# Output product of the first block: the first attention's part in all four blocks ahead of the second's

## The chip, the core and the metric

The kernel runs on one core of a Trainium2 chip. The metric is the device time of one execution in microseconds (us). The core has five engines that run side by side, each through its own list of instructions in order: TensorE (PE, matrix products), VectorE (DVE), ScalarE (ACT), GpSimd (POOL) and SyncE (SP, which issues the transfers). They wait for each other by semaphores.

## The reference

The reference is two transformer blocks in float32 over 256 positions of width 1024. The change lies in the first block:

```python
h = rmsnorm(x, g_mix_pre[l])
proj = h @ w_in[l]
...
y_fox = forgetting_attention(...)            # first attention, 512 columns
y_chk = chunked_relpos_attention(...)        # second attention, 512 columns
y = jnp.concatenate([rmsnorm(y_fox.reshape(B, S, D_FOX), g_fox_out[l]),
                     rmsnorm(y_chk.reshape(B, S, D_CHK), g_chk_out[l])], axis=-1)
x = x + rmsnorm(y @ w_out[l], g_mix_post[l])
h = rmsnorm(x, g_mem_pre[l])
mem_n = rmsnorm(mem, g_mem_kv[l])
y = memory_cross_attention(h, mem_n, w_mq, w_mk, w_mv, w_mo)   # four heads of width 256
x = x + rmsnorm(y, g_mem_post[l])
```

A feed-forward part (1024 to 4096 to 1024) follows, and then the second block (a gated delta rule, a sparse attention, a feed-forward part).

## The kernel before

The 256 positions are two halves of 128, since an engine works on 128 partitions. Every float32 product is made of three products in a faster format: both operands are split into a high and a low part (`whi`, `wlo` for weights, `xhi`, `xlo` for activations), and `mm3` adds high x high, high x low and low x high in one bank of TensorE's accumulator. Weights come in units of 512 KB (class `Part`): SyncE loads a unit into `raw`, ScalarE casts it to `whi`, VectorE subtracts to `wlo`. A unit of w_out is 256 rows by 512 columns, so w_out has eight units; the first four give columns 0 to 511 of the output, the others columns 512 to 1023. In each four, the first two hold the rows of the first attention and the last two those of the second.

The order on each engine is that in which the Python code writes the instructions. The main line writes products; after each `mm3` or so it calls `tick`, which lets side chains (generators, class `Side`) write their next piece. When a chain may go on is decided by the planner's own clock (`k.clock`, `k.at`, `k.done`: estimated costs). A chain that the planner thinks is ready is written; `k.finish(...)` writes what is left of the named chains at once, whatever the clock says. `part` and `drop` take the next unit or let one go, and write casts and splits of later units up to a limit (`pump`); `k.held` counts the units kept for the other half.

Around the change the main line writes, in this order: `gemm_t` for the memory keys; the first half of the memory values (`gn`, columns 0 to 511); the output product (`gs`, the loop that the change rewrites); the second half of the memory values (`gn` again, four units, 48 matmuls); `k.finish(*st.values())` (line 1024); the query product `gemm_t(k, ht, D, mq_evac)` (`gt`, 192 matmuls); `k.finish(*[st[i] for i in range(3)])` (line 1071); the memory output product (`mo`).

In the output product the two attentions are not yet normalized: their parts of a block go to two banks, and `out_sum` (line 988) scales and adds them: `y` = bank of the first attention x its factor (ScalarE), then + bank of the second x its factor (VectorE). When a half has both column blocks, `out_post` (line 996) starts `chain_post` (line 467): sums of squares of y on ScalarE (`junk`), `yg` = y x gain, the factor `rs` on GpSimd, `x` = yg x rs + old x, sums of squares of x (`junk`), `xg` = x x gain, `rs`, `xg` x rs, and then eight transposes on TensorE in two banks (`tb`), each cast to `xhi` by ScalarE and split to `xlo` by VectorE. This is the query product's moving operand, and that needs both halves.

The loop before goes half by half and block by block: first attention, second attention, first attention, second attention. The second attention's chain is finished (`k.finish(s_chk)`) after the first two units of the first block. In the query product each of the four heads starts a chain `mem_head` (line 1030) when its columns are there: for each half the scores (`ms`), maximum, exponential, sum, scaling (`mp`), two transposes (`tb`), a copy (`mpt`); then the head's output (`ops`), cast and split.

Of the kernel before, what the change touches and what calls it, by code (L numbers as in the profile page):

```python
# [16 lines left out]
P = 128  # L17
S = 256
D = 1024
# [343 lines left out]
    return [Part(w, r, 2, c0 + c, wd) for c in range(0, ncols, wd) for r in range(0, D, S)]  # L363


def gemm_t(k, xt, ncols, evac):

    for i in range(ncols // 256):
        ps = k.bank((P, 2, S), "gt")
        for m in range(2):  # L370
            p = k.part()
            for kt in range(KT):
                k.mm3(ps[:, m, :], p.at(kt, 0, P), xt.x(kt), kt == 0, kt == KT - 1)
                k.tick()
            if m == 1 and not evac(i, ps):
                k.put()
            k.tick()
# [11 lines left out]
def gemm_n_inter(k, xt, evac, width=512, nb=1):  # L389

    ps = [[k.bank(name="gn") for _ in range(nb)] for _ in range(2)]
    for i in range(4):
        p = k.part()
        for half in range(2):
            mm_n(k, ps[half], xt, half, p, 2 * i, width)
            if i == 3 and not evac(half, ps[half]):
                k.put(nb)
    k.tick()
# [134 lines left out]
def ffn(k, xt, before_b, evac, last=None):  # L533
# [24 lines left out]
    def up(c):  # L558
        u_tiles(c)
        uh, ul = us[c]  # L560

        def ev(i, ps):
            r = k.t2([P, 2, S], name="r")
            sl = slice(2 * i, 2 * i + 2)
            nc.scalar.activation(r, ps, AF.Relu)
            nc.vector.tensor_tensor(r, r, r, op=OP.mult)
            split(k, uh[:, sl], ul[:, sl], r)
        gemm_t(k, xt, 512, ev)
# [98 lines left out]
def join(sides):  # L667

    if sides:
        yield list(sides)  # L670
# [20 lines left out]
def block1(k, x, mem, w_in, b_fgt, rel, g_fox_out, g_chk_out, w_out, g_mix_pre, g_mix_post,  # L691
           g_mem_kv, w_mq, w_mk, w_mv, w_mo, g_mem_pre, g_mem_post, w_ff1, w_ff2, g_ff_pre,
           g_ff_post, next_gain, xt_next, before_ffn=None):
    nc = k.nc

    x0 = [k.t4([P, D], name="x0") for _ in range(2)]
    grow = k.t4([1, D], name="grow")
# [12 lines left out]
    for half in range(2):  # L710
        xg.append(k.t4([P, D], name="xg"))
        ss, r = k.small(1, "ss"), k.small(1, "rs")
# [4 lines left out]
    u = k.units  # L717
# [91 lines left out]

    fq, ev = qk_evac(0.125)  # L810
    gemm_t(k, ht, 512, ev)
    mt = XT(k)
    s_m = [k.add(chain_norm(k, mt, half, m0[half], gkv)) for half in range(2)]
    fk, ev = qk_evac(1.0)
    gemm_t(k, ht, 512, ev)


    yt = XT(k)
# [143 lines left out]
    s_chk = k.add(chk())  # L962
# [23 lines left out]
    st = {}  # L986

    def out_sum(half, j, banks, y):

        yield banks + [rso]  # L990
        yy = y[:, j * 512:j * 512 + 512]
        nc.scalar.activation(yy, banks[0], AF.Copy, scale=rso[:, 0, half:half + 1])
        nc.vector.scalar_tensor_tensor(yy, banks[1], rso[:, 1, half:half + 1], yy, op0=OP.mult, op1=OP.add)
        k.put(2)

    def out_post(half, sums, y):
        yield from join(sums)
        yield from chain_post(k, half, [y[:, :512], y[:, 512:]], gpo, x0[half], x1[half], gmp, ht, nbanks=0)

    parts = []  # L1000
    for half in range(2):
        y, sums = k.t4([P, D], name="y"), []
        for j in range(2):
            banks = []
            for i in range(4):
                if half == 0:
                    parts.append(k.part())
                    k.held += 1
                else:
                    k.drop()  # L1010
                if i % 2 == 0:
                    banks.append(k.bank(name="gs"))
                if (half, j, i) == (0, 0, 2):
                    k.finish(s_chk)
                p = parts[4 * j + i]
                for r in range(2):
                    k.mm3(banks[i // 2], yt.x(2 * i + r, half), p.at(r, 0, 512), i % 2 == 0 and r == 0,
                          i % 2 == 1 and r == 1)
                    k.tick()
            sums.append(k.add(out_sum(half, j, banks, y), rank=-1))  # L1020
        st[half] = k.add(out_post(half, sums, y), rank=-1)
        k.tick()
    gemm_n_inter(k, mt, lambda half, ps: nc.scalar.copy(mv[half][:, 1], ps[0]))
    k.finish(*st.values())

# [36 lines left out]
    st = {}  # L1062
# [12 lines left out]
    parts = {}  # L1075
# [863 lines left out]
```

## Time and profile before

| | us |
|---|---|
| median of 3 runs | 886.81 (886.73 to 886.85) |
| the profiled execution | 886.64 |
| its span, first to last instruction | 884.9 |
| TensorE busy | 871.4 (98%) |
| VectorE busy | 597.7 (68%) |
| ScalarE busy | 456.5 (52%) |
| GpSimd busy | 88.9 (10%) |

TensorE has 89% of the chain of waits that ended last, VectorE 5%, ScalarE 4%. The output product takes 144 to 167 us of the span, the second half of the memory values 167 to 178, the query product with most of the heads 180 to 216. A matmul's end in the profile is modelled and its successor starts before it, so the pace of a series is read from the starts. In a timeline row stand the start, the time busy, the engine, the line of the code, the operation, the result and the operands, the sizes, the count, and in brackets the idle time before it with what ended it. Most vector instructions are written through one helper, so their line is 96; matmuls are written in line 212, transposes in line 225.

### The profile page before, as it was taken

What the parts mean: (1) busy time and instruction counts of PE and PEld (TensorE: products, weight loads), DVE (VectorE), ACT (ScalarE), POOL (GpSimd) and SP (SyncE); (2) the same over time, 40 slices, a digit from 0 to 9 for tenths busy, and PEclk for the clock granted to TensorE, in tenths of its full rate; (3) what the DMA queues carried; (4) which work ended last, traced back from release to release, by engine and by line L of the source; (5) the groups of instructions that cost most, each with busy time, mean ns of one, the idle gap of its engine ahead of it and who ended that gap; (6) DMA issues with size and microseconds to landing.
All of it is one profiled execution on the core that took longest, in us unless ns stands there. A gap on an engine that the chain in (4) does not pass through costs nothing.

```text
span 884.9 us, 14527 instructions
## 1 busy us (share of the span) xinstructions
PE 871.4 (98%) x5664; PEld 766.8 (87%) x5664; DVE 597.7 (68%) x1074; ACT 456.5 (52%) x775; POOL 88.9 (10%) x144
## 2 busy tenths in 40 slices
PE   8999999999999999999999999999999999999998
PEld 7978987888789999998798899988987889999987
DVE  5686674865687556554769999878579785555541
ACT  6665644653476444442656665554564654444440
POOL 3100000200020000000100038800010000000000
PEclk9999999999999999999999999999999999999999
DMA  8982455472387666654651677385126587666621
GB/s 265 303 220 78 138 180 176 144 259 80 94 240 221 207 196 191 189 191 145 170 161 49 191 172 198 89 245 168 49 72 197 169 248 217 178 194 187 196 82 47
DMA packets 163381, 150.32 MB, mean 170 GB/s; under 512 B 21105, under 2 KB 128241, under 8 KB 163314
## 3 DMA queue, kind: packets, MB, share of 16 engines
q1 hardware_dynamic: 162738, 148.36, 56.7%
q10 hardware_dynamic: 576, 1.05, 0.4%
q8 instruction: 44, 0.72, 0.3%
q14 instruction: 23, 0.19, 0.1%
HBM read 147.56 MB, written 1.84 MB: 169 GB/s over the span
## 4 chain that ended last, share of the span: by engine, by line
PE 89%; DVE 5%; ACT 4%; issue 1%; DMA 0%; POOL 0%; DVEq 0%; ACTq 0%; POOLq 0%
PE gt L212 33%; PE acc L212 20%; PE gs L212 13%; PE gn L212 9%; PE tb L225 3%; PE mo L212 3%; DVE wlo L96 2%; ACT whi L96 1%; PE s L212 1%; ACT junk L96 1%; PE ops L212 1%; ACT p L96 1%; PE ms L212 1%; PE o L212 1%; DVE Z L96 1%
## 5 line engine op out<-in xcount | busy, mean ns | idle before, releaser
L96 DVE TENSOR_TENSOR wlo<-raw,whi 128x1024 fp32r<-128x1024 f32 (+1 forms) x263 | 315.2, 1224 | 107.2 <-ACT whi L96 106.6
L96 ACT CAST whi<-raw 128x1024 fp32r<-128x1024 f32 (+1 forms) x264 | 268.2, 1047 | 81.6 <-DMA raw<-in_w_in_dram 29.3
L212 PE MATMUL gt<-xhi,whi 128*128 128x256 f32 x832 | 238.5, 287 | 0.2 <-ACT xhi L96 0.2
L212 PE MATMUL gt<-xlo,whi 128*128 128x256 f32 x832 | 233.6, 281 | 0.3 <-DVE xlo L96 0.3
L212 PE MATMUL gt<-xhi,wlo 128*128 128x256 f32 x832 | 233.2, 280 | 0.0
L212 PEld LDWEIGHTS gt<-xhi,whi 128*128 128x128 f32 x832 | 156.7, 188 | 4.1 <-issue 3.2
L212 PEld LDWEIGHTS gt<-xlo,whi 128*128 128x128 f32 x832 | 156.8, 188 | 1.0 <-DVE xlo L96 0.5
L212 PEld LDWEIGHTS gt<-xhi,wlo 128*128 128x128 f32 x832 | 156.7, 188 | 0.0
L212 PE MATMUL acc<-whi,ul 128*128 128x512 f32 (+1 forms) x288 | 106.2, 369 | 0.0
L212 PE MATMUL acc<-wlo,uh 128*128 128x512 f32 (+1 forms) x288 | 106.2, 369 | 0.0
L212 PE MATMUL acc<-whi,uh 128*128 128x512 f32 (+1 forms) x288 | 106.1, 368 | 0.0
L212 PE MATMUL gs<-whi,xhi 128*128 128x512 f32 (+1 forms) x208 | 80.4, 387 | 0.5 <-ACT xhi L96 0.5
L212 PE MATMUL gs<-whi,xlo 128*128 128x512 f32 (+1 forms) x208 | 79.0, 380 | 0.4 <-DVE xlo L96 0.4
L212 PE MATMUL gs<-wlo,xhi 128*128 128x512 f32 (+1 forms) x208 | 78.7, 379 | 0.1
L212 PE MATMUL gn<-whi,xhi 128*128 128x512 f32 x160 | 67.3, 420 | 0.0
L212 PE MATMUL gn<-whi,xlo 128*128 128x512 f32 x160 | 63.0, 394 | 0.0
L212 PE MATMUL gn<-wlo,xhi 128*128 128x512 f32 x160 | 63.0, 394 | 0.0
L212 PEld LDWEIGHTS acc<-whi,ul 128*128 128x128 f32 x288 | 54.1, 188 | 9.8
L212 PEld LDWEIGHTS acc<-whi,uh 128*128 128x128 f32 x288 | 54.2, 188 | 9.6
L212 PEld LDWEIGHTS acc<-wlo,uh 128*128 128x128 f32 x288 | 54.1, 188 | 9.6
L96 DVE TENSOR_TENSOR r<-r 128x512 f32<-128x512 f32 x32 | 22.1, 690 | 58.4 <-ACT r L96 58.4
L96 ACT ACTIVATE r<-gt 128x512 f32<-128x512 f32 x24 | 14.4, 598 | 74.7 <-PE gt L212 74.7
(367 smaller groups left out, 1123.4 us busy)
## 6 DMA issues: line engine op xcount, KB each, us to landing
raw<-in_w_in_dram SPq DMA_DIRECT2D x84, 512.0 KB, 4.8
raw<-in_w_ff_dram SPq DMA_DIRECT2D x64, 512.0 KB, 5.0
raw<-in_w_mlp_up_dram SPq DMA_DIRECT2D x32, 512.0 KB, 5.7
raw<-in_w_mlp_down_dram SPq DMA_DIRECT2D x32, 512.0 KB, 4.3
raw<-in_w_out_dram SPq DMA_DIRECT2D x16, 512.0 KB, 3.8
raw<-in_w_mk_dram SPq DMA_DIRECT2D x8, 512.0 KB, 4.7
raw<-in_w_mv_dram SPq DMA_DIRECT2D x8, 512.0 KB, 3.6
raw<-in_w_mq_dram SPq DMA_DIRECT2D x8, 512.0 KB, 4.9
```

The lines of the kernel that those rows point to most:

```text
L96: f(*args, **kw)
L212: self.nc.tensor.matmul(out, lhsT, rhs, start=start, stop=stop)
L225: self.nc.tensor.transpose(out, in_, self.ident[:n, :n])
```

## The change

The loop over halves and blocks is now inside a loop over the two attentions: for the first attention (t = 0) all four pairs of half and column block, 48 matmuls, then `k.finish(s_chk)`, then for the second (t = 1) the same four. The banks of the first pass stay occupied until their sums. The eight units of w_out are loaded in the order of their new use (0, 1, 4, 5, 2, 3, 6, 7). A unit is held from its first half to its second, so four at a time instead of eight.

```diff
+def first_rows_first(units, w):
+
+    at = [i for i, u in enumerate(units) if u.src.tensor is w.tensor]
+    part = [units[i] for i in at]
+    for i, j in zip(at, (0, 1, 4, 5, 2, 3, 6, 7)):
+        units[i] = part[j]
...
     nc = k.nc
+    first_rows_first(k.units, w_out)
...
-    parts = []
-    for half in range(2):
-        y, sums = k.t4([P, D], name="y"), []
-        for j in range(2):
-            banks = []
-            for i in range(4):
-                if half == 0:
-                    parts.append(k.part())
-                    k.held += 1
-                else:
-                    k.drop()
-                if i % 2 == 0:
-                    banks.append(k.bank(name="gs"))
-                if (half, j, i) == (0, 0, 2):
-                    k.finish(s_chk)
-                p = parts[4 * j + i]
-                for r in range(2):
-                    k.mm3(banks[i // 2], yt.x(2 * i + r, half), p.at(r, 0, 512), i % 2 == 0 and r == 0,
-                          i % 2 == 1 and r == 1)
-                    k.tick()
-            sums.append(k.add(out_sum(half, j, banks, y), rank=-1))
-        st[half] = k.add(out_post(half, sums, y), rank=-1)
-        k.tick()
+
+    parts, banks, ys, sums = {}, {}, {}, {}
+    for t in range(2):
+        if t == 1:
+            k.finish(s_chk)
+        for half in range(2):
+            if t == 1:
+                ys[half], sums[half] = k.t4([P, D], name="y"), []
+            for j in range(2):
+                banks[t, half, j] = k.bank(name="gs")
+                for i in range(2):
+                    if half == 0:
+                        parts[t, j, i] = k.part()
+                        k.held += 1
+                    else:
+                        k.drop()
+                    for r in range(2):
+                        k.mm3(banks[t, half, j], yt.x(4 * t + 2 * i + r, half), parts[t, j, i].at(r, 0, 512),
+                              i == 0 and r == 0, i == 1 and r == 1)
+                        k.tick()
+                if t == 1:
+                    sums[half].append(k.add(out_sum(half, j, [banks[0, half, j], banks[1, half, j]], ys[half]),
+                                            rank=-1))
+            if t == 1:
+                st[half] = k.add(out_post(half, sums[half], ys[half]), rank=-1)
+            k.tick()
```

The change moves the instructions of the chains behind it as well, since the planner writes them when its clock says so. On VectorE, from the second sum of half 1 to the scaling before its transposes, stood this before (`x0_75`, `y_1865` and `xg_2033` are half 1's; `tb_1971` holds half 0's second four transposes):

```order
L96 TENSOR_TENSOR xlo_1791<-tb_1971,xhi_1789 128x4x128
L96 SCALAR_TENSOR_TENSOR y_1865<-gs_1951,rso_639,y_1865 128x512
L96 TENSOR_TENSOR wlo_2001<-raw_1910,whi_2000 128x1024
L96 TENSOR_TENSOR yg_2012<-y_1865,gain_1684 128x512 x2
L96 SCALAR_TENSOR_TENSOR x0_75<-yg_2012,rs_2020,x0_75 128x512 x2
L96 TENSOR_TENSOR xg_2033<-x0_75,gain_1686 128x512 x2
L96 TENSOR_TENSOR wlo_2037<-raw_1926,whi_2036 128x1024
L96 TENSOR_TENSOR wlo_2059<-raw_1943,whi_2058 128x1024
L96 TENSOR_SCALAR xg_2033<-xg_2033,rs_2056 128x512 x2
```

and on the same engine stands this now (`y_1903` and `xg_2035` are half 1's, `xg_1940`, `tb_2010` and `tb_2041` half 0's):

```order
L96 SCALAR_TENSOR_TENSOR y_1903<-gs_1943,rso_639,y_1903 128x512
L96 TENSOR_SCALAR xg_1940<-xg_1940,rs_1971 128x512 x2
L96 TENSOR_TENSOR wlo_1987<-raw_1860,whi_1986 128x1024
L96 TENSOR_TENSOR yg_2004<-y_1903,gain_1684 128x512 x2
L96 TENSOR_TENSOR wlo_2020<-raw_1874,whi_2019 128x1024
L96 TENSOR_TENSOR xlo_1790<-tb_2010,xhi_1788 128x4x128
L96 SCALAR_TENSOR_TENSOR x0_75<-yg_2004,rs_2017,x0_75 128x512 x2
L96 TENSOR_TENSOR xg_2035<-x0_75,gain_1686 128x512 x2
L96 TENSOR_TENSOR xlo_1791<-tb_2041,xhi_1789 128x4x128
L96 TENSOR_TENSOR wlo_2055<-raw_1923,whi_2054 128x1024
L96 TENSOR_SCALAR xg_2035<-xg_2035,rs_2076 128x512 x2
```

Half 0's scaling and its two `xlo` stood ahead of half 1's second sum and now stand behind it, among half 1's own instructions.

On ScalarE, in the same stretch, half 1's two y copies stood before among casts, apart from half 0's `junk` passes over x:

```order
L96 ACTIVATE junk_96,ss_1891<-x0_74 128x512 x2
L96 CAST whi_1906<-raw_1772 128x1024
L96 CAST whi_1922<-raw_1797 128x1024
L96 ACTIVATE y_1865<-gs_1866,rso_639 128x512
L96 CAST whi_1939<-raw_1844 128x1024
L96 CAST xhi_1788<-tb_1958 128x4x128
L96 CAST whi_1978<-raw_1857 128x1024
L96 CAST xhi_1789<-tb_1971 128x4x128
L96 ACTIVATE y_1865<-gs_1928,rso_639 128x512
L96 CAST whi_2000<-raw_1910 128x1024
L96 ACTIVATE junk_96,ss_2009<-y_1865 128x512 x2
L96 ACTIVATE junk_96,ss_2028<-x0_75 128x512 x2
```

and now:

```order
L96 CAST whi_1919<-raw_1835 128x1024
L96 ACTIVATE junk_96,ss_1935<-x0_74 128x512 x2
L96 ACTIVATE y_1903<-gs_1824,rso_639 128x512
L96 CAST whi_1960<-raw_1848 128x1024
L96 ACTIVATE y_1903<-gs_1843,rso_639 128x512
L96 CAST whi_1986<-raw_1860 128x1024
L96 ACTIVATE junk_96,ss_2001<-y_1903 128x512 x2
L96 CAST whi_2019<-raw_1874 128x1024
L96 CAST xhi_1788<-tb_2010 128x4x128
L96 ACTIVATE junk_96,ss_2030<-x0_75 128x512 x2
L96 CAST xhi_1789<-tb_2041 128x4x128
L96 CAST whi_2054<-raw_1923 128x1024
```

The two copies now stand directly behind half 0's passes over x, and half 0's casts to `xhi` among half 1's passes. Ahead of half 0's y copies ScalarE now has five weight casts in a row.

On TensorE, at the end of the query product, the last pieces of heads 1 and 2 stood so before (24 `gt` matmuls between `ms` and the last `tb`, of which the first three are shown):

```order
L212 MATMUL ops<-mpt,mv 128x256 x4
L225 MATMUL tb<-ident,mp 128x128 x2
...
L212 MATMUL ms<-mk,mq 128x256 x2
L212 MATMUL gt<-xhi,whi 128x256
L212 MATMUL gt<-xlo,whi 128x256
L212 MATMUL gt<-xhi,wlo 128x256
...
L225 MATMUL tb<-ident,mp 128x128 x2
L212 MATMUL ops<-mpt,mv 128x256 x4
```

and stand so now:

```order
L212 MATMUL ops<-mpt,mv 128x256 x4
L212 MATMUL ms<-mk,mq 128x256 x2
L212 MATMUL gt<-xhi,whi 128x256
L212 MATMUL gt<-xlo,whi 128x256
L212 MATMUL gt<-xhi,wlo 128x256
L225 MATMUL tb<-ident,mp 128x128 x2
L212 MATMUL ops<-mpt,mv 128x256 x4
```

The scores of head 2's second half (`ms`) now stand three `gt` matmuls ahead of the transposes that need their softmax, where 24 were between.

## Rows read from the trace of the kernel before

**Rows 1.** What TensorE waited for, 124 to 246 us: total, times, longest.

```profile
PE ssp L212 <- DVE sqo L96: 1.2, 1, 1.2
```

**Rows 2.** Timeline of TensorE, 144 to 181 us: start, us, engine, operation.

```profile
144.06 0.40 PE L212 MATMUL gs<-whi,xhi 128*128 128x512 f32 x1
...
164.64 0.39 PE L212 MATMUL gs<-whi,xlo 128*128 128x512 f32 x1
...
178.02 0.40 PE L212 MATMUL gn<-whi,xlo 128*128 128x512 f32 x1
...
178.78 1.09 PE L225 MATMUL tb<-ident,xg 128*128 128x128 f32 x8 [0.36 <-DVE xg L96]
...
180.84 0.38 PE L212 MATMUL gt<-xlo,whi 128*128 128x256 f32 x1 [0.34 <-DVE xlo L96]
```

**Rows 3.** Timeline of VectorE, 155 to 179 us.

```profile
155.41 0.75 DVE L96 SCALAR_TENSOR_TENSOR y<-gs,rso,y 128x512 f32<-128x512 f32 x1 [2.51 <-PE gs L212]
...
168.22 0.68 DVE L96 TENSOR_TENSOR xlo<-tb,xhi 128x512 fp32r<-128x512 f32 x1
168.82 0.74 DVE L96 SCALAR_TENSOR_TENSOR y<-gs,rso,y 128x512 f32<-128x512 f32 x1
169.48 1.23 DVE L96 TENSOR_TENSOR wlo<-raw,whi 128x1024 fp32r<-128x1024 f32 x1
170.63 1.28 DVE L96 TENSOR_TENSOR yg<-y,gain 128x512 f32<-128x512 f32 x2
172.68 1.41 DVE L96 SCALAR_TENSOR_TENSOR x<-yg,rs,x 128x512 f32<-128x512 f32 x2 [0.77 <-POOL rs L96]
174.01 1.28 DVE L96 TENSOR_TENSOR xg<-x,gain 128x512 f32<-128x512 f32 x2
...
178.25 0.88 DVE L96 TENSOR_SCALAR xg<-xg,rs 128x512 f32<-128x512 f32 x2
```

**Rows 4.** Timeline of ScalarE, 167 to 174 us.

```profile
167.34 0.59 ACT L96 CAST xhi<-tb 128x512 fp32r<-128x512 f32 x1 [0.29 <-PE tb L225]
167.82 0.69 ACT L96 ACTIVATE y<-gs,rso 128x512 f32<-128x512 f32 x1
168.40 1.05 ACT L96 CAST whi<-raw 128x1024 fp32r<-128x1024 f32 x1
169.34 0.64 ACT L96 ACTIVATE junk<-y 128x512 bf16<-128x512 f32 x1
...
170.10 0.63 ACT L96 ACTIVATE junk<-y 128x512 bf16<-128x512 f32 x1
...
173.52 0.63 ACT L96 ACTIVATE junk<-x 128x512 bf16<-128x512 f32 x1 [2.69 <-DVE x L96]
```

**Rows 5.** Timeline of TensorE, then of VectorE, 207 to 214 us.

```profile
207.16 1.89 PE L212 MATMUL ops<-mpt,mv 128*128 128x256 f32 x8
...
208.89 0.38 PE L225 MATMUL tb<-ident,mp 128*128 128x128 f32 x2
...
209.47 1.03 PE L212 MATMUL ms<-mk,mq 128*128 128x256 f32 x4
...
210.15 0.47 PE L212 MATMUL gt<-xhi,whi 128*128 128x256 f32 x1
...
213.60 0.41 PE L225 MATMUL tb<-ident,mp 128*128 128x128 f32 x2 [0.33 <-DVE mp L96]
...
210.32 0.41 DVE L96 COPY mpt<-tb 128x256 f32<-128x256 f32 x1
...
211.80 0.42 DVE L96 TENSOR_REDUCE nmx<-ms 128x1 f32<-128x256 f32 x1
```

**Rows 6.** The granted clock in 40 slices; timeline of TensorE, 7 to 13 us.

```profile
PEclk9999999999999999999999999999999999999999
...
7.44 3.68 PE L225 MATMUL tb<-ident,xg 128*128 128x128 f32 x16 [0.51 <-DVE xg L96]
...
12.00 0.42 PE L212 MATMUL gs<-whi,xlo 128*128 128x260 f32 x1
```

## The prediction

> **What bounds the kernel now.** I read the page first, then TensorE's waits in the stretch from 124 to 246 us, then the timelines of TensorE, VectorE and ScalarE around the edit. TensorE sets the time: every later stage is queued behind it in one order, so a microsecond that it waits here is a microsecond at the end. The first question is whether it waits where the change is made. It does not. The only wait that belongs to the second attention is that of its sum-of-squares product, 1.2 us for `sqo` [rows 1], and it ends at 138.69 us, inside the product before the output product. From the first `gs` matmul at 144.06 to the one at 164.64 there are 89 steps in 20.58 us, 0.2312 us each, with no gap [rows 2]. So reordering these 96 matmuls can win nothing among them.
>
> The place that can move is the end of this stage. The memory value product `gn` issues its last matmul at 178.02 and would hand over at 178.25 (178.02 + 0.23); the eight transposes of the second half's new input start at 178.78, and the query product runs evenly only from 180.84 [rows 2]. These transposes wait for a chain on VectorE, ScalarE and GpSimd (sum, norm, residual, norm, scale), which ends in the `xg` scaling at 178.25 [rows 3]. What TensorE waits for last here is that chain: from 178.25 to 180.84 are 2.59 us, of which the transposes need 1.09 and the first query matmul 0.11; about 1.4 is waiting.
>
> **The change, part by part.**
>
> *The order of the 96 matmuls.* Same count, same 0.2312 us: nothing. The weights do not hold it up: the units are loaded and split in the order of their use, one per six matmuls as before, and there was no gap for one. If this cover failed, a split (1.23 us [rows 3]) would show as a gap among the `gs`. Cost 0.
>
> *When the halves are complete.* Before, half 0 is complete after 48 matmuls and its second sum starts on VectorE at 155.41 [rows 3]. Now it is complete after 72: 24 x 0.2312 = 5.55 us later, 160.96. Half 1 is complete after 96, as before, 0.4 us earlier even, since the transposes of half 0 no longer stand among the products. So two chains that ran one after the other (half 0's from 155.4, half 1's from 166.9) now overlap, on two in-order engines. I walk through the new order with the steps, start to next start, of [rows 3, 4]: VectorE y 0.66, weight split wlo 1.15, yg pair 1.28, x pair 1.33, xg pair 1.28, xlo 0.60, scaling pair 0.87 in the middle of work; ScalarE y 0.58, whi 0.94, each junk 0.76.
>
> Half 0 first. Sum at 160.96 (0.75 busy), yg to 162.9. ScalarE's second junk pass over y runs from 161.8 to 162.5, the weight cast behind it (1.05) ends at about 163.6, and the weight split, which now stands ahead of the x pair, ends at 164.75. Without that split the x pair would have started 2.71 us after the sum (172.68 - 168.82, less the one split 1.15 in it [rows 3]), at 163.7; it loses 1.1. It runs to 166.08, xg to 167.36. ScalarE's junk passes over x end at 167.08, and only there does it reach half 1's y copies, whose products were ready long before: the wait added by the new order is theirs, behind `junk`. y copy, cast, y copy: 167.08, 167.66, 168.60, 169.18. VectorE takes half 1's first sum at 167.8, a split to 169.88, and the second sum at 169.88. Before, that second sum stood at 168.82 [rows 3]. So half 1's chain starts 1.06 us later.
>
> Then from the second sum to the scaling that the transposes need: before 178.25 - 168.82 = 9.43 us. Now there stand between them the scaling of half 0 (0.79), a split (1.15), yg (1.28), a split (1.15), half 0's xlo (0.60), x (1.33), xg (1.28), half 0's second xlo and a last split. The sum up to xg, with y itself, is 8.24, so xg ends at 178.12. The second xlo waits for ScalarE, whose junk passes over x come first (x start 175.51 + 0.84 + 2 x 0.76 = 177.87, then 0.59 for the cast): 178.45 to 179.05. The last split waits 0.3 for its cast and ends at 180.52. There the scaling starts, against 178.25: **2.3 us late**. GpSimd is not on this path: x follows the second junk of y by 1.85 us at most (170.10 + 0.73 to 172.68 [rows 3, 4]), which gives 173.5, and x starts at 175.5. TensorE reaches the same point at the same 178.25 (the two sets of transposes move from among `gs` to among `gn`), so the whole 2.3 is waited. The transposes of half 0 stand after 24 `gn` matmuls, at 171.8, and their input is ready at 171.0: no wait there. Behind the waiting transposes stand all 192 matmuls of the query product.
>
> Bounds: if VectorE never waited from 160.96 on, its own work in the new order (the steps above, five splits among them) is 17.6 us and the scaling would start at 178.5, 0.3 late. The walk has four waits of 2.0 us together; if each took as long as the longest that VectorE has in these rows, 0.77 for `rs` [rows 3], they would be 3.1 and the scaling 3.4 late. I take 2.3, from the walk, which is built on rows of the same operations.
>
> *The memory heads.* The planner places their small products among the query product's 192 matmuls, and the new order of the stage before shifts its clock. Its last pieces are forced out at the end of the product by the call that finishes heads 0 to 2. Before, the score product of head 2's second half (`ms` at 209.47) has 24 `gt` matmuls between it and its transposes at 213.60, which then wait 0.33 by the modelled ends, about 0.5 by the starts [rows 5]. Now only 3 stand between. With the durations of [rows 5]: from the start of head 1's `ops` TensorE needs 1.73 for them, 0.68 for `ms` (209.47 to 210.15) and about 0.5 for three `gt` (the first takes 0.47, the others stand close behind), 2.9 in all. The transposes need the softmax: VectorE is through with head 1's split of `ops` 3.16 after their start (210.32 - 207.16), and from the maximum to the transposes pass 1.80 (213.60 - 211.80), 4.96 in all. That is 2.1 waited against 0.5, **1.6 us more**. I find no other head that waits by more than 0.2. Bounds: 0, if the earlier heads run so far ahead that the tail hides as before; 2.7, if one weight split more (1.15) stands in VectorE's way there.
>
> *Rest.* SyncE's loads and GpSimd's instructions stand in the same order as before, only which unit of w_out comes third has changed; TensorE waits for none of them. From the memory output product on, every engine's order is the same as before. Sum: 2.3 + 1.6 = 3.9 us on the profiled 886.64 (span 884.9 and 1.7 around it), 890.5; the median of the runs stands 0.17 above the profiled one, so 890.7.
>
> *A rule against it.* A 128x260 matmul at 12.00 us takes 0.42 us, where a 128x512 one at 144.06 takes 0.40 [rows 2, 6]: TensorE ran at its lower level, 1.2 GHz, after the opening waits, and at 2.4 GHz later. The granted clock shows 9 or more tenths in every slice, even the first [rows 6], so the durations are the better witness; and the 0.40 at 144.06 comes 5.4 us after the 1.2 us wait. The Trainium skill (TensorE: Matmul & The Clock Gate, section "Why this matters for your kernels") says that idle gaps between bursts of matmuls can throw the clock back to half. By that rule the sum would grow by the price in the third rival; by the row it does not. The trace has no wait of the length that I forecast after the opening, so it neither confirms nor refutes the rule, and the sum stays.
>
> **The rivals.**
>
> *Only the chain is late.* If the tail of the heads hides, 886.8 + 2.3 = 889.1. For it: the planner put the pieces where by its own clock they were ready. Against it: the three `gt` are forced, not planned. 0.16.
>
> *Only the heads cost.* If VectorE closes its waits, 886.8 + 0.3 + 1.6 = 888.7; with nothing of the chain left, 888.4. 0.08.
>
> *The half-pace clock.* After the opening TensorE worked without a break from its transposes at 7.44 and was still at the low level at 12.00 [rows 6]: some 4.8 us of work that lost half, 2.4 us. If the wait at 178.25, 2.8 us with the 0.5 of before, throws it back once, 890.7 + 2.4 = 893.1. For it, the pace at the opening; against it, the full pace soon after the 1.2 us wait. 0.07.
>
> *The other side: half 1's chain is earlier.* Its last product ends 0.4 us sooner, and five weight casts now stand ahead of half 0's copies, out of its way. If ScalarE makes half 1's copies as the products end, the sum starts at 166.6, and after the 9.43 of before the scaling starts at 176.0, ahead of 178.25: the 1.4 us of waiting around the transposes go, and the time is 885.4, or 887.0 with the heads' 1.6: not slower. It decides at the second sum: it must start before 168.3. Against it: in ScalarE's queue the copies stand behind half 0's junk passes. 0.10, and in a third of these the heads' stall of 0.5 goes too and the time falls below 885.0.
>
> *The change does not do what it says.* That needs the second attention to be late for the product; its wait ends 5.4 us ahead [rows 1, 2]. It changes no number: the cost is in the chains either way. 0.01, at 886.8.
>
> **How the numbers follow.** The forecast has 0.58, at 890.7. A measurement of this kernel can tell about 0.2% (1.8 us) from no change, so slower means above 888.6: the forecast, the chain alone and the clock, 0.58 + 0.16 + 0.07 = 0.81. Faster is a third of the other side, 0.03. The rest, 0.16, is the same. The range goes from 888.4 (only the heads) to 892.6 (chain 3.4 and heads 2.4, short of their end of 2.7); its own range for the likeliest is 889.6 to 892.
>
> **What would show it.** Right: in the profile after, the transposes at the end of `gn` wait 2 to 3 us for `xg`, starting near 181; VectorE's half-1 second sum near 169.9; head 2's last transposes wait about 2 us for `mp`; from the memory output product on a constant shift. Wrong: a gap among the `gs` matmuls, transposes of half 1 before 179, or a shift that shrinks after 246 us.

## The result, and the profile after

The changed kernel takes 893.48 us, the median of 5 runs (893.14 to 894.16), against 886.81 before (886.69 to 887.25): ratio 1.0075, 95% interval 1.006 to 1.009. It is slower, as forecast, but by 6.7 us and not by 3.9, and 0.9 us above the range. The profiled execution took 893.48 with a span of 891.7, 6.8 more than before.

The first view is what TensorE waited for, 124 to 246 us of the changed kernel (total, times, longest).

```profile
PE tb L225 <- DVE xg L96: 2.7, 1, 2.7
PE tb L225 <- DVE mp L96: 1.8, 1, 1.8
PE ssp L212 <- DVE sqo L96: 1.2, 1, 1.2
...
```

Both waits that the prediction named are there: 2.7 for `xg` (0.36 before [rows 2]) and 1.8 for `mp` (0.33 before [rows 5]). The wait for `sqo` is the 1.2 of [rows 1], untouched. These two lines hold 3.7 us of new waiting, and 6.8 are lost. TensorE's timeline of the changed kernel shows the rest.

```profile
143.90 0.40 PE L212 MATMUL gs<-whi,xhi 128*128 128x512 f32 x1
...
177.87 0.40 PE L212 MATMUL gn<-whi,xlo 128*128 128x512 f32 x1
180.93 1.06 PE L225 MATMUL tb<-ident,xg 128*128 128x128 f32 x8 [2.66 <-DVE xg L96]
182.23 0.58 PE L212 MATMUL gt<-xhi,whi 128*128 128x256 f32 x1 [0.24 <-ACT xhi L96]
...
183.34 0.41 PE L212 MATMUL gt<-xhi,wlo 128*128 128x256 f32 x1
183.55 0.41 PE L212 MATMUL gt<-xhi,whi 128*128 128x256 f32 x1
...
189.01 0.28 PE L212 MATMUL gt<-xhi,wlo 128*128 128x256 f32 x1
189.13 0.28 PE L212 MATMUL gt<-xhi,whi 128*128 128x256 f32 x1
...
192.26 1.02 PE L212 MATMUL ms<-mk,mq 128*128 128x256 f32 x4
...
219.90 0.44 PE L225 MATMUL tb<-ident,mp 128*128 128x128 f32 x2 [1.76 <-DVE mp L96]
220.85 1.99 PE L212 MATMUL ops<-mpt,mv 128*128 128x256 f32 x8 [0.52 <-DVE mpt L96]
...
251.15 0.39 PE L212 MATMUL gs<-whi,xhi 128*128 128x512 f32 x1
```

The `gt` matmuls of 256 columns follow each other every 0.21 us up to 188.88, and every 0.12 from there on. The granted clock in stretches of the same trace says why (columns: stretch, its sum; busy time and count of PE, PEld, DVE, ACT and POOL; granted clock, DMA share, GB/s).

```profile
178.00:180.80 2.80, 0.27 (x2) 0.00 (x0) 2.34 (x4) 2.10 (x4) 0.72 (x2) 1.00 0.03 9
180.80:182.00 1.20, 1.06 (x8) 0.86 (x8) 0.38 (x1) 0.41 (x1) 0.00 (x0) 1.00 0.31 65
182.00:188.50 6.50, 6.13 (x27) 5.83 (x28) 5.92 (x6) 4.46 (x6) 0.00 (x0) 0.50 1.02 323
188.50:190.00 1.50, 1.50 (x13) 1.50 (x13) 0.00 (x0) 0.00 (x0) 0.00 (x0) 0.87 0.94 333
```

Behind the wait the clock falls from its upper level (1.00, 2.4 GHz) to the lower one (0.50, 1.2 GHz), for 6.8 us in all. Such a drop is called a fall from here on. The mean clock of an execution tells of it too: 6.8 us at half pace in 892 make a mean of 0.996, 3.4 us one of 0.998. Before the fall TensorE had done nothing from 178.3 to 180.9, and then eight transposes with a pause behind them. To put a price on it, here are three rows of TensorE's timeline of the kernel before, that the prediction did not need: the first `gt`, the first `ms`, and the first `gs` of the feed-forward part.

```profile
180.11 0.38 PE L212 MATMUL gt<-xhi,whi 128*128 128x256 f32 x1 [0.24 <-ACT xhi L96]
...
187.51 1.02 PE L212 MATMUL ms<-mk,mq 128*128 128x256 f32 x4
...
244.85 0.39 PE L212 MATMUL gs<-whi,xhi 128*128 128x512 f32 x1
```

Read as shifts of the starts:

| TensorE's row | before | after | shift |
|---|---|---|---|
| first `gs` | 144.06 | 143.90 | -0.16 |
| transposes of half 1 | 178.78 | 180.93 | +2.15 |
| first `gt` | 180.11 | 182.23 | +2.12 |
| first `ms`, 57 matmuls later | 187.51 | 192.26 | +4.75 |
| first `gs` of the feed-forward part | 244.85 | 251.15 | +6.30 |

The chain cost 2.15 + 0.16 = 2.31, the clock 4.75 - 2.12 = **2.63**, and the heads and their tail 6.30 - 4.75 = 1.55. From there to the end the shift goes down to 6.0 and up to 6.8.

VectorE's timeline in the changed kernel, to be held against [rows 3]:

```profile
167.44 0.75 DVE L96 SCALAR_TENSOR_TENSOR y<-gs,rso,y 128x512 f32<-128x512 f32 x1 [0.32 <-ACT y L96]
...
169.52 0.75 DVE L96 SCALAR_TENSOR_TENSOR y<-gs,rso,y 128x512 f32<-128x512 f32 x1
...
178.21 0.69 DVE L96 TENSOR_TENSOR xlo<-tb,xhi 128x512 fp32r<-128x512 f32 x1 [0.22 <-ACT xhi L96]
179.16 1.23 DVE L96 TENSOR_TENSOR wlo<-raw,whi 128x1024 fp32r<-128x1024 f32 x1 [0.25 <-ACT whi L96]
180.30 0.88 DVE L96 TENSOR_SCALAR xg<-xg,rs 128x512 f32<-128x512 f32 x2
```

And ScalarE's, against [rows 4]:

```profile
166.10 0.63 ACT L96 ACTIVATE junk<-x 128x512 bf16<-128x512 f32 x1
...
166.74 0.67 ACT L96 ACTIVATE y<-gs,rso 128x512 f32<-128x512 f32 x1
...
168.25 0.69 ACT L96 ACTIVATE y<-gs,rso 128x512 f32<-128x512 f32 x1
```

Half 1's y copies stand behind half 0's last `junk`, and the scaling of half 1 starts at 180.30 instead of 178.25. The walk had 180.52.

### The profile page after: what moved, and what is told of

Same layout as the page of the kernel before. It is cut to its first block, busy times and chain, and to the rows that moved or that the text cites. A ratio compares the mean times of both kernels' runs of the same rounds, so it can differ in the third digit from the quotient of the medians.

```text
span 891.7 us, 14531 instructions
## 1 busy us (share of the span) xinstructions
PE 874.3 (98%) x5664; PEld 770.0 (86%) x5664; DVE 598.0 (67%) x1074; ACT 456.6 (51%) x775; POOL 90.3 (10%) x144
## 4 chain that ended last, share of the span: by engine, by line
PE 86%; DVE 6%; ACT 5%; issue 1%; POOL 1%; DMA 0%; DVEq 0%; ACTq 0%; POOLq 0%
PE gt L212 32%; PE acc L212 20%; PE gs L212 12%; PE gn L212 9%; PE tb L225 3%; PE mo L212 3%; DVE wlo L96 2%; ACT whi L96 1%; ACT junk L96 1%; PE s L212 1%; ACT p L96 1%; PE ops L212 1%; ACT xhi L96 1%; PE ms L212 1%; DVE xlo L96 1%
```

## The experiments

What was open: whether the low clock is a consequence of the wait, and how much of the 6.7 us each of the three parts carries. The runs of the kernel before that belong to the experiments have medians of 886.71 to 886.92.

**The wait made by hand in the kernel before.** Two operations, and for the second run one, on a dead tile ahead of half 1's scaling (`late` is 0 in every other chain; in the second run the last line has `1 * half`):

```diff
     yield rs
+    for _ in range(late):
+        k.nc.vector.eng.tensor_tensor(yg, yg, yg, op=OP.max)
     yield from chain_xt(k, xt, half, [c(xg, 0), c(xg, 1)], rs)
...
+                              late=2 * half)
```

> The kernel before, with two VectorE operations of 128 x 1024 elements (about 1.15 us each, by the weight splits of this size) that copy a dead tile onto itself, ahead of half 1's scaling of 'xg' in the chain behind the output product; the output and every other instruction's place are the same. This does by hand to the kernel before what the change did by order: half 1's transposes come 2.3 us late, with TensorE idle for 2.6 us ahead of them. Theory (the wait costs itself and throws the clock to half pace): 886.8 + 2.3 + 2.6 = 891.7 us, and the granted clock falls to 0.5 for 6 to 7 us behind the wait. Rival (a wait costs only itself): 889.1, with the clock at 1.00. Rival (the change's own order hides something that the kernel before doesn't have): 889.1 with whatever clock.

Measured: 891.27 us (890.72 to 891.70), ratio 1.0049 (1.0037 to 1.0061). TensorE's timeline in the kernel with two:

```profile
178.29 0.40 PE L212 MATMUL gn<-whi,xlo 128*128 128x512 f32 x1
181.45 1.97 PE L225 MATMUL tb<-ident,xg 128*128 128x128 f32 x8 [2.76 <-DVE xg L96]
```

Its busy times and granted clock by stretches (columns as above; the clock is the third from the right):

```profile
178.00:180.80 2.80, 0.69 (x3) 0.20 (x2) 2.77 (x3) 0.59 (x1) 0.00 (x0) 0.99 0.69 200
180.80:182.20 1.40, 0.75 (x4) 0.75 (x5) 0.99 (x3) 0.00 (x0) 0.00 (x0) 0.50 1.08 288
...
186.00:188.00 2.00, 2.00 (x13) 2.00 (x12) 2.00 (x3) 1.83 (x2) 0.00 (x0) 0.60 0.34 100
```

A wait as long as the changed kernel's, in the old order, brings the low clock with it: 4.4 us for 2.4 of waiting. The clock is down at 180.8, while TensorE still stands and before the transposes begin. The change's order is not needed for it.

> The kernel before, with one VectorE operation of 128 x 1024 that copies a dead tile onto itself ahead of half 1's scaling; half the dose of the run with two, which made TensorE wait 2.76 us, threw the clock to half for 6.8 us and cost 4.35. The output is the same. Theory (only a long wait throws the clock): TensorE waits about 1.55 us, the clock stays at 1.00 and the time is 886.9 + 1.2 = 888.1 us. Rival (any wait above a fraction of a us at this place throws the clock, as the wait of 2.09 us in the run with early copies did for 3.4 us): 889.4 to 890.7, with a fall behind the wait.

Measured: 888.05 us (887.76 to 890.21, 11 runs), ratio 1.0018 (1.0009 to 1.0027). TensorE's timeline in the profiled execution:

```profile
180.09 1.09 PE L225 MATMUL tb<-ident,xg 128*128 128x128 f32 x8 [1.50 <-DVE xg L96]
...
182.37 0.28 PE L212 MATMUL gt<-xhi,wlo 128*128 128x256 f32 x1
182.49 0.28 PE L212 MATMUL gt<-xhi,whi 128*128 128x256 f32 x1
```

Half the dose (one operation) costs about its own wait, and the steps are 0.12 at once. Eight of the 11 executions took 887.76 to 888.27 with a mean clock of 1.000, 1.3 us more than before at their median, for 1.14 of added waiting. The other three had 0.998 and took 889.34 to 890.21, 1.3 to 2.2 us longer than those eight. So at a wait of 1.5 the fall comes in some executions only (where it lay in those three was not seen), and in one and the same kernel the price goes with the clock.

**The wait of the changed kernel filled with work.** If the idle time is the cause, matmuls that nobody needs must keep the clock up.

```diff
     gemm_n_inter(k, mt, lambda half, ps: nc.scalar.copy(mv[half][:, 1], ps[0]))
+    warm = k.psp.tile([P, 512], F32, name="warm", tag="b")
+    for i in range(12):
+        k.nc.tensor.matmul(warm, mt.x(0, 0)[0], flat(mt.hi[0][:, 0:2]), start=i == 0, stop=i == 11)
     k.finish(*st.values())
```

> The changed kernel, with twelve more matmuls of 128 x 512 (12 x 0.23 = 2.8 us by the trace of the changed kernel) that write to a bank nobody reads, placed behind the last 'gn' matmul and ahead of half 1's transposes; the output is the same. TensorE's 2.66 us of idle time there is filled with work, and nothing else moves: half 1's transposes still wait for VectorE's scaling. Theory (the granted clock fell to 0.5 because TensorE stood idle for 2.66 us, and the 6.83 us at half pace cost 2.6 us): the granted clock stays at 1.00 through 178 to 190 us, the transposes start at the same 180.9 us or up to 0.3 later, and the median is 890.7 to 891.2 us. Rival (the low clock comes from something else at that place, as the burst of transfers at 182 to 189 us or the transposes themselves): the clock falls all the same and the median stays at 893.5. Second rival (the low clock costs nothing, the 2.6 us are a wait elsewhere): the clock stays up and the median is still 893.5.

Measured: 892.63 us (891.78 to 893.29), 0.85 below the changed kernel and not 2.6. The trace tells why. TensorE's timeline:

```profile
178.15 2.92 PE L1038 MATMUL warm<-xhi 128*128 128x512 f32 x12
180.91 1.07 PE L225 MATMUL tb<-ident,xg 128*128 128x128 f32 x8
...
189.54 1.02 PE L212 MATMUL ms<-mk,mq 128*128 128x256 f32 x4
...
218.19 0.44 PE L225 MATMUL tb<-ident,mp 128*128 128x128 f32 x2 [1.76 <-DVE mp L96]
219.15 3.61 PE L212 MATMUL ops<-mpt,mv 128*128 128x256 f32 x8 [0.52 <-DVE mpt L96]
```

And the stretches behind the two waits, with the granted clock:

```profile
182.20:186.00 3.80, 3.46 (x27) 3.26 (x28) 3.65 (x5) 3.80 (x5) 0.00 (x0) 1.00 1.07 307
...
219.00:222.50 3.50, 3.35 (x9) 2.72 (x9) 0.10 (x1) 0.00 (x0) 0.00 (x0) 0.51 0.00 0
```

At the place of the first fall the clock stays at 1.00, with the transposes as late as ever (180.91) and the transfers as dense (307 GB/s in the first row, 323 in the changed kernel): the first `ms`, behind the same 57 `gt`, starts at 189.54 instead of 192.26, 2.7 earlier. That refutes the rival that blames the transfers or the transposes. But now the clock falls at 219, behind the heads' wait of 1.76 us, which in the changed kernel's profile had no fall behind it: the same eight `ops` take 3.61 instead of 1.99. With one more wait, of 0.81 for `mp` at 195 us, that the changed kernel does not have, the 2.7 are gone again at the end of the heads (first `gs` of the feed-forward part at 251.13 against 251.15). No transfer runs in the stretch of the second fall (0 GB/s). All five executions had a mean clock of 0.998.

**The heads put back.** The planner is told the landing times that it reckons in the kernel before, which puts the memory heads into that kernel's order:

```diff
+    for u, at in zip(k.units[k.n_split + 2:k.n_dma], (0.91, 2.65)):
+        for s in spans(u.raw):
+            k.done[s] = k.clock + at
+    k.at["dma"] = k.clock + 4.126
     gemm_t(k, ht, D, mq_evac)
```

> The changed kernel, but the planner is told at the start of the query product of the memory attention that the next two weight units land as late as it had reckoned for the kernel before (0.58 and 4.2 us later than it reckons here). By that the memory heads, and all that follows, stand in the same order as in the kernel before; the output product and half 1's chain stay as in the changed kernel. Theory (the heads' new places cost 1.6 of the 6.7 us): 891.9 us, with the wait of 'tb' for 'mp' at head 2 back from 1.8 to about 0.3 us. Rival (the heads cost nothing in the end, the time is all in the chain and the clock): 893.5. Other rival (the heads' cost depends on the slow clock ahead of them): anything between.

Measured: 890.98 us (890.95 to 891.64), 2.5 less than the changed kernel; expected 1.6. TensorE's wait for `mp` is the 0.3 of before again. Not all of the 2.5 belongs to the heads, as the first `ms` shows:

```profile
191.05 1.02 PE L212 MATMUL ms<-mk,mq 128*128 128x256 f32 x4
```

It starts 1.2 us earlier than in the changed kernel, though everything up to there stands in the same order: the fall lasted 3.4 us in this profile instead of 6.8. That leaves 1.3 for the heads.

> Both edits at once in the changed kernel: the twelve matmuls that fill TensorE's wait ahead of half 1's transposes, and the planner told of the later landings, so that the memory heads stand as in the kernel before. The output is the same. Theory (the change costs 2.3 us of waiting at the chain, 2.6 us at half pace behind it and 1.6 us at the heads; in the run with the filled wait alone a second fall of the clock, at 219 us behind the heads' wait of 1.8 us, took its place): with both gone only the lateness of the chain is left, 886.9 + 2.3 = 889.2 us, with no fall of the clock. Rival (the falls of the clock are by chance or by the span of time, and one comes whatever waits are there): 890.5 to 891.5 with a fall somewhere before 250 us.

Measured, with both edits: 889.01 us (888.71 to 890.48, 7 runs), ratio 1.0028 (1.0017 to 1.0039), with a mean clock of 1.000 in all seven. The stretch behind the filled wait in the profile:

```profile
182.20:190.00 7.80, 7.24 (x60) 6.80 (x60) 5.92 (x6) 5.35 (x7) 0.00 (x0) 1.00 1.00 295
```

What is left is the late chain alone: 889.01 - 886.71 = 2.3 us, the term as forecast. (The profiled execution is the slowest of the seven, 890.48: it is 0.6 us late ahead of the output product already and loses another 0.7 near 590 us, so the price is read from the median.) The rival by which a fall comes in any case is out.

> The kernel before, with the planner told at the start of the query product of the memory attention that the next two weight units land as early as it reckons in the changed kernel; by that the memory heads stand in the changed kernel's order, and the output product and its chain as before. The output is the same. Theory: the heads' 1.6 us, so 888.5 us; with no low clock ahead of it the wait of 1.8 us at head 2 throws the clock to half pace in some or all executions, as it did where the first wait was filled, which adds 1.5 to 1.9: 890.0 to 890.4 in those. Rival (the heads' places cost nothing without the late chain): 886.9. Rival (a wait under 2 us doesn't move the clock when nothing fell before it): 888.5 in all executions with the mean clock at 1.000.

The same edit the other way round, the heads of the changed kernel in the kernel before (0.91, 2.65, 4.126 become -3.25, 2.07, 3.542). Measured: 890.39 us (888.86 to 890.93), ratio 1.0038 (1.0025 to 1.0052). Two executions with the mean clock at 1.000 took 888.86 and 889.21, the three at 0.998 took 890.39 to 890.93. So the heads cost 2.2 to 2.5 without a fall, somewhat over the 1.6 that the trace of the changed kernel gives up to 251 us (here the shift is 1.8 at 255 us and grows to 2.5 by the end, in many small steps; I can't name those), and about 4 with one. The profiled execution is one of the first two, so it is the mean clock alone that puts the fall in the other three.

**Why half 1's chain is late.** Two runs. In the first, ScalarE takes the first attention's part of y out of its bank early, so that it no longer stands behind half 0's `junk`:

```diff
+    def out_first(half, j, bank, y):
+        yield [bank, rso[:, 0]]
+        nc.scalar.activation(y[:, j * 512:j * 512 + 512], bank, AF.Copy, scale=rso[:, 0, half:half + 1])
+        k.put()
...
-        nc.scalar.activation(yy, banks[0], AF.Copy, scale=rso[:, 0, half:half + 1])
-        nc.vector.scalar_tensor_tensor(yy, banks[1], rso[:, 1, half:half + 1], yy, op0=OP.mult, op1=OP.add)
+        nc.vector.scalar_tensor_tensor(yy, bank, rso[:, 1, half:half + 1], yy, op0=OP.mult, op1=OP.add)
...
```

> The changed kernel, with the first attention's part of y copied out of its bank by ScalarE as soon as that bank is done (from about 146 us), so that no copy of half 1 stands behind half 0's chain; the output is the same. The memory heads stand as in the changed kernel. Theory (half 1's chain is late because its copies stand behind half 0's statistics): the scaling of half 1's 'xg' starts 1 to 1.6 us earlier than 180.30, TensorE waits about 1.2 us and the granted clock stays at 1.00: 889 to 890 us. Rival (the chain is late by VectorE's own queue, in which half 0's scaling and the weight splits stand ahead): the scaling stays within 0.5 us of 180.30, the clock falls again, 892.8 to 893.5.

Measured: 893.74 us (891.27 to 894.88). VectorE's timeline in this kernel:

```profile
168.88 0.74 DVE L96 SCALAR_TENSOR_TENSOR y<-gs,rso,y 128x512 f32<-128x512 f32 x1
169.54 0.88 DVE L96 TENSOR_SCALAR xg<-xg,rs 128x512 f32<-128x512 f32 x2
...
172.67 0.69 DVE L96 TENSOR_TENSOR xlo<-tb,xhi 128x512 fp32r<-128x512 f32 x1
...
178.65 1.22 DVE L96 TENSOR_TENSOR wlo<-raw,whi 128x1024 fp32r<-128x1024 f32 x1
179.78 0.88 DVE L96 TENSOR_SCALAR xg<-xg,rs 128x512 f32<-128x512 f32 x2
```

The theory missed and its rival is nearly right. The copies are out of the way, and the second sum comes 0.64 earlier (168.88), but the scaling only 0.52: half 0's scaling and `xlo`, and the weight splits, stand among half 1's steps as before. The wait was 2.09 us. In the profiled execution the clock fell behind it, for 3.4 us, and once more at 219 behind the heads; of the six executions two had a mean clock of 1.000, and they took 891.27 and 891.80, the others 893.70 to 894.88.

In the second, the change is made within each half alone, so that half 0 is done early again:

```diff
-    for t in range(2):
-        if t == 1:
-            k.finish(s_chk)
-        for half in range(2):
+    for half in range(2):
+        for t in range(2):
+            if (half, t) == (0, 1):
+                k.finish(s_chk)
...
```

> The change within each half alone: half 0 takes the first attention's part of both blocks and then the second's, and half 1 after it likewise, with the weight units in the changed kernel's order. The output is the same. Half 0 is done as early as in the kernel before, 24 matmuls earlier than in the changed kernel, so its chain is out of the way when half 1's copies come. Theory (the cost is that half 0 is done late and its chain collides with half 1's; the order of the two attentions as such costs nothing): 886.5 to 887.2 us, TensorE's wait for 'xg' within 0.3 of 0.36 us, no fall of the clock. Rival (later y copies of the first attention's part by themselves make half 1's chain late): 888 to 891.

Measured: 887.00 us (886.41 to 888.21, 11 runs), ratio 1.0004 (0.9995 to 1.0013): no difference clear of the noise. TensorE waits 0.45 for `xg`, and in VectorE's timeline the two halves' scalings stand apart, with half 1's sums between them:

```profile
163.48 0.88 DVE L96 TENSOR_SCALAR xg<-xg,rs 128x512 f32<-128x512 f32 x2
165.40 0.74 DVE L96 SCALAR_TENSOR_TENSOR y<-gs,rso,y 128x512 f32<-128x512 f32 x1
168.46 0.74 DVE L96 SCALAR_TENSOR_TENSOR y<-gs,rso,y 128x512 f32<-128x512 f32 x1
177.90 0.87 DVE L96 TENSOR_SCALAR xg<-xg,rs 128x512 f32<-128x512 f32 x2
```

The order of the two attentions as such costs nothing that these runs can tell. What costs is that half 0 is complete only after 72 of the 96 matmuls.

**A version that beats both.** In the kernel before, the heads' tail waits 0.33 us for `mp` [rows 5], 0.52 for `mpt`, and 0.68 for head 3's `xhi`. The memory output product can start with heads 0 and 1 and take the others as they come:

```diff
-    k.finish(*[st[i] for i in range(3)])
+    k.finish(st[0], st[1])
...
-        for js, iis in ((0, (0, 1, 2)), (1, (0, 1, 2)), (0, (3,)), (1, (3,))):
-            if iis == (3,):
-                k.finish(st[3])
+        for js, iis in ((0, (0, 1)), (1, (0, 1)), (0, (2,)), (1, (2,)), (0, (3,)), (1, (3,))):
+            if len(iis) == 1:
+                k.finish(st[iis[0]])
```

> The kernel before, with the memory attention's output product in another order: it starts when heads 0 and 1 are done, with their six matmuls for each of the two banks of half 0, and takes heads 2 and 3 as they are done; before, it began when heads 0 to 2 were done. The output is the same. TensorE's waits of 0.33 us for 'mp' and 0.52 us for 'mpt' ahead of the first 'mo' are covered by these matmuls, with their pauses around the transposes. Theory: 1.0 to 1.2 us less than before, 885.7 to 885.9 us. Rival (head 3's softmax comes later in this order, and its wait ahead of the last 'mo' of the half, 0.68 us now, grows by what the others save): 886.9.

Measured in the kernel before: **884.26 us** (884.10 to 884.72, 7 runs), ratio 0.9971 (0.9960 to 0.9982), 2.45 less. More than forecast, since the wait of 0.68 for head 3 went too, with its pauses: head 3's pieces now come earlier among the matmuls. None of the three waits is left.

> The changed kernel, with the memory attention's output product started when heads 0 and 1 are done, as in the run of the kernel before with that edit (884.26 us, 2.45 less). The output is the same. The heads' wait of 1.8 us is covered by matmuls of that product; the late chain and the low clock behind it stay. Theory (2.3 of chain, 2.6 of clock, and the heads' cost gone): 884.3 + 4.1 to 4.9 = 888.4 to 889.2 us. Rival (the heads' new places cost as much in another wait, as that of the last 'mo' for head 3): 890.5 to 891.0.

Measured in the changed kernel: 890.08 us (888.92 to 890.91), between theory and rival. TensorE waits for `mp` no longer, but 0.75 for `mpt` and 0.68 for `xhi` at head 3, so the rival is half right; the wait for `xg` is 2.64, and the clock falls behind it. The one execution with a mean clock of 1.000 took 888.92.

> The kernel before with that order of the memory output product, and with the two small matmuls that sum the second attention's squares ('ssp') planned 1.6 us later, behind nine more 'gn' matmuls; the output is the same. TensorE waits 1.23 us for VectorE's sums ahead of them in the kernel before. Theory (that wait is covered by the matmuls that stand behind it): 884.3 - 1.2 = 883.1 us. Rival (half 1's chain behind the output product is bound by VectorE's queue, so that TensorE's wait for 'xg' grows from 0.36 by the 1.2 us that the product comes earlier): 884.3, with a wait of about 1.5 us there.

The last kernel adds to the better one a delay in the planner's account for the second attention's `ssp` (`if t == 1: yield 1.6` ahead of its bank). Measured: **882.95 us** (882.64 to 883.74), ratio 0.9959 (0.9947 to 0.9972), 3.8 less than before. TensorE's timeline where the 1.2 of [rows 1] was:

```profile
139.07 0.40 PE L212 MATMUL gn<-whi,xlo 128*128 128x512 f32 x1
139.31 0.50 PE L212 MATMUL ssp<-ones,sqo 128*128 128x1 f32 x4
```

No wait, and the one for `xg` has stayed at 0.36 although the output product comes 1.5 earlier: the chain behind the output product follows TensorE there and is not bound by VectorE's queue, as the rival had it.

## Why the prediction was right or wrong

*The 96 matmuls, cost 0:* right. The series has the same step and no gap, and the run with the order within each half shows no cost of the order alone that is clear of the noise.

*The halves' chains, 2.3 us:* right in place and size. The rows of VectorE answer to the walk within 0.4 us at each step (second sum forecast 169.88, measured 169.52; scaling 180.52 and 180.30); the chain cost 2.31 by the shifts, and with the two other parts taken away by experiment 2.3 us remain. The reason that the walk gave, ScalarE's copies behind `junk`, is the smaller part of it: with the copies early the scaling came only 0.5 sooner. Of the 2.05 us by which the scaling is late, 0.70 had arisen at the second sum (169.52 against 168.82) and 1.35 arose behind it. The larger part is thus half 0's steps and the splits in VectorE's queue, which the walk had counted but not named as the cause. The walk put 1.06 on the first and 1.2 on the second.

*The memory heads, 1.6 us:* right in place, and near in size: 1.55 by the shifts of the trace, 1.3 by the kernel with the heads put back, 2.2 to 2.5 by executions without a fall of the kernel with that part alone.

*"The sum stays":* this is the step that failed. Under "A rule against it" the clock was costed at 0, since no row before showed a wait of this length after the opening and the full pace returned soon after the 1.2 us wait. The wait of 2.7 us that the sum itself forecast was outside what that row could answer for. The clock fell in each of the changed kernel's runs (mean 0.996 in all five; 0.999 or 1.000 in every execution of the kernel before whose clock is on record) and cost 2.63 us. That is close to the 2.4 of the third rival, which had been given 0.07, but the closeness is luck: that price was half of the 4.8 us at the low level in the opening, while the falls in the profiles last 3.4 or 6.8 us, and one of 3.4 costs about 1.3 (kernel with the heads put back: `gt` to `ms` 8.67 us against 7.40). The row on the opening [rows 6] shows half pace in TensorE's first 12 us, with no full pace ahead of it; it could price the low level, but not show that a wait brings it. So no row spoke against a fall behind 2.7 us, and the term belonged in the range. The Trainium skill (TensorE: Matmul & The Clock Gate, section "HAM oscillation — how this bites in real kernels") describes the pattern, a wait between bursts after which the next burst runs at half pace. The changed kernel's trace agrees with the pattern (0.21 us per `gt` behind the wait, 0.12 later), but the waits that the section tells of are longer than the 2.1 to 2.8 us that did it here; the measurement decides. The sum is 2.3 + 2.6 + 1.6 = 6.5 us, less the 0.16 by which the stage starts earlier; the rest of the 6.7 comes in small steps behind 251 us and is not explained.

*The rivals:* the other side, half 1's chain earlier, failed at the point named: the second sum came at 169.52, not before 168.3. The cost of the heads alone and of the chain alone were each measured apart, and neither is the whole.

*The range:* its upper end, 892.6, was worked out from the chain and the heads, and left the clock outside. A forecast that makes TensorE wait for 2 to 3 us, longer than any wait that the trace has behind its opening, should have put the price of the low level into the range.

## What to carry to other kernels

When a change makes TensorE wait for more than it has so far, price the wait twice: its length, and the pace of the matmuls behind it, read from any place in the trace where TensorE stood as long. Look at when the work on each half is complete, not at the order within it: two chains that ran one after the other collide on the in-order engines when the first is completed late. Where a planner places small products, cover their softmax with matmuls that are ready (here the next product's first units); that paid 2.45 us, where neither order of the large ones that was run paid anything.

## What was not expected of the hardware

A wait of 2.1 to 2.8 us threw the granted clock to 0.5 in every profile that has one (four kernels beside the changed one), for 6.8 us in two (the changed kernel and the one with two added operations) and 3.4 in three, most of it with TensorE back at work. It does not do so in every execution: two of six with the early copies and one of five of the changed kernel with the new output product had a mean clock of 1.000. What decides between the lengths is open, and it is not the order of the instructions: the changed kernel and the one with the heads put back have the same order up to the fall, and by the mean clock one kernel shows both (with two added operations 0.996 in four executions and 0.998 in one; with the heads put back 0.998 in four and 0.996 in one). Waits of 1.5 to 1.8 us did it in some executions of the same kernel and not in others, and the changed kernel's second wait, of 1.76 us, passed without a fall 31 us after the first one had ended, while the same wait brought one where the first had been prevented, and one also in the kernel with early copies, 34 us behind its first. What decides there is open too. Filling the first wait gave back 0.85 us and not the 2.6 that its fall had cost: the next wait had a fall instead. The 1.2 us wait for `sqo` had no fall behind it in any profile.
